# Output projection in two parts: attention heads first, recurrence heads second, in a two-layer fp32 trunk on one core

## The chip, the cores and the metric

One core of a Trainium2 chip runs the whole program as one launch. The metric is the device time in microseconds (us), as a median over runs. PE is the matrix engine, with PEld its weight loads; DVE, ACT and POOL are the vector, scalar and GpSimd engines; SP issues all the DMAs of this kernel.

## The reference

Two layers. In each, the normed input goes through one projection into four attention heads and four gated-recurrence heads. Their outputs, each normed per head, are laid side by side and go through one output projection that is added to the residual; a squared-ReLU MLP follows.

```python
for l in range(DEPTH):                         # DEPTH 2, S = D = 1024
    h = rms_norm(x, norm1_g[l])
    z = h @ w_in[l]                            # split into aq ak av | rq rf ri rg
    oa = diff_attention(...)                   # 4 heads x 128 columns
    orr = hgrn2_chunked(...) * silu(rg)        # 4 heads x 128 columns
    mixed = concatenate([oa, orr], axis=-1)
    x = x + mixed @ w_out[l]                   # the step that is changed
    h2 = rms_norm(x, norm2_g[l])
    u = relu(h2 @ w_up[l])
    x = x + (u * u) @ w_down[l]
return rms_norm(x, final_g)
```

## The kernel before

Everything is held with the model dimension on the 128 partitions: eight blocks `b` of 128 features by two halves `hf` of 512 tokens. A product of fp32 precision is made from three matmuls on split numbers (`hi` and `lo` parts, names `hh`, `hl` for activations, `whi`, `wlo` for weights), so `dense` (L146) with eight blocks is 24 matmuls of 128x512 into one PSUM bank. Those banks come from a pool with the tag `mm`, which has two buffers. `weights` loads a 512 KB piece into `wst` (three buffers), ACT rounds it to `whi` (L130), DVE makes `wlo` (L132), at high priority.

The heads run in pairs, attention head h and then recurrence head h. A scheduler orders the instructions of each engine before the launch, by priority (program order, high priority for evacuations and weights) and its own estimate of when operands are there; at run time each engine takes its list in that order and waits where an operand is missing. So the last attention head and the last recurrence head (`hgrn` with h = 3, output block 7, constant `LAST`) are interleaved. The result of each head goes to DRAM (`mx`), except block 7, which is split at once (L316, L317).

Then comes the output projection. For each half it loads the seven blocks of `mx` into `wst`, splits them into the tiles `hh`, `hl` that the normed input had used, loads the residual blocks `xt[b][hf]` from DRAM (`xs`), and makes eight groups of 24 matmuls, in the block order 0, 4, 1, 5, 2, 6, 3, 7. Each group is added to the residual tile by one DVE instruction (L858). The residual tiles lie in the pool `x`, which is opened after the attention's pool (`actx`) has been closed and takes its memory. After each half comes `norm_rows` (squares on ACT, L188, their sum on DVE, L189, a matmul with ones, L205, an inverse root, giving `R`), and then the scaling (L865) and splitting (L549, L550) of the eight blocks for the MLP, whose first products are the plain ones of `up_plain` (L647): half 0 first, half 1 next.

Of the kernel before, what the change touches and what calls it, by code (L numbers as in the profile page):

```python
# [15 lines left out]
ALU = mybir.AluOpType  # L16
# [4 lines left out]
P = 128  # L21
# [3 lines left out]
NB = D // P  # L25
HALF = 512
NH = 4
# [10 lines left out]
LAST = 2 * NH - 1  # L38
# [7 lines left out]
def trunk(ctx, tc, x, norm1_g, w_in, lam_qk, attn_norm_g, lb_logits, hgrn_norm_g,  # L46
# [3 lines left out]
    V, A, G, T = nc.vector, nc.scalar, nc.gpsimd, nc.tensor  # L50
    dma = nc.sync.dma_start
# [10 lines left out]
    def pst(tag="pa"):  # L62
        return psp.tile([P, HALF], F32, tag=tag, name=tag, bufs=3)
# [11 lines left out]
    xt = {}  # L75
    first = []

    def load_w(src, shape):
        st = wp.tile([P, 1024], F32, tag="wst", name="wst", bufs=3)
        dma(st.rearrange("p (a c) -> p a c", c=shape[1]), src)  # L80
        return st

    with tc.high_priority():
        dma(ident, c_ident)
        dma(rows[0:16], norm1_g.rearrange("l (b p) -> (l b) p", p=P))
        for hf in range(2):
            for dh in range(2):
                t = xp.tile([P, 4, HALF], F32, tag="xt", name="xt", bufs=4)
# [22 lines left out]
    xs = dram.tile([P, NB, S], F32, name="xs")  # L111
# [3 lines left out]
    def h_tiles(b, hf):  # L115
        hi = hp.tile([P, HALF], F32R, tag=f"hh{b}_{hf}", name=f"hh{b}_{hf}")
        lo = hp.tile([P, HALF], F32R, tag=f"hl{b}_{hf}", name=f"hl{b}_{hf}")
        return hi, lo
# [7 lines left out]
    def weights(src, shape, eng=V):  # L126
        with tc.high_priority():
            st = first.pop(0) if first else load_w(src, shape)
            hi = wp.tile([P, 1024], F32R, tag="whi", name="whi")
            A.copy(hi, st)  # L130
            lo = wp.tile([P, 1024], F32R, tag="wlo", name="wlo")
            eng.tensor_tensor(lo, st, hi.bitcast(F32), op=ALU.subtract)  # L132
        r = lambda t: t.rearrange("p (a c) -> p a c", c=shape[1])
        return r(hi), r(lo)

    def dense(w, hs, evac, halves=(0, 1), order=None):
        whi, wlo = w
        order = order or list(range(len(hs)))
        for hf in halves:
            ps = mmp.tile([P, HALF], F32, tag="mm", name="mm")  # L140
            n = 3 * len(order)
            i = 0
            for b in order:
                hi, lo = hs[b][hf]
                for lt, rt in ((whi, hi), (whi, lo), (wlo, hi)):
                    T.matmul(ps, lt[:, b], rt, start=(i == 0), stop=(i == n - 1))  # L146
                    i += 1
            with tc.high_priority():
                evac(hf, ps)
# [86 lines left out]
    for hf in range(2):  # L236
# [6 lines left out]
        for b in range(NB):  # L243
            ps = pst("pa" if b % 2 else "pr")
# [67 lines left out]
    ms = {}  # L312

    def split(src, b, hf):
        hi, lo = h_tiles(b, hf)
        A.copy(hi, src)  # L316
        V.tensor_tensor(lo, src, hi.bitcast(F32), op=ALU.subtract)  # L317
        ms[b, hf] = (hi, lo)
# [445 lines left out]
    for l in range(DEPTH):  # L764
        wl = w_in[l].rearrange("(b p) c -> p b c", p=P)
        rctx, actx, xctx, mctx = ExitStack(), ExitStack(), ExitStack(), ExitStack()
# [5 lines left out]
        for h in range(NH):  # L772
            ap = apool
            Lq = [ap.tile([P, S], F32R, tag=f"L{m}", name=f"L{m}") for m in range(2)]
            Rk = [ap.tile([P, S], F32R, tag=f"R{m}", name=f"R{m}") for m in range(2)]

            def evq(hf, ps):
                sl = slice(hf * HALF, (hf + 1) * HALF)
                t = half(ap, "ta", 1)
                V.tensor_tensor(t, ps, R1[hf], op=ALU.mult)  # L780
                for m in range(2):
                    a, b = slice(64 * m, 64 * m + 64), slice(64 - 64 * m, 128 - 64 * m)
                    A.activation(Lq[m][a, sl], t[a], AF.Copy, scale=-0.125)
                    V.scalar_tensor_tensor(Lq[m][b, sl], t[a], -0.125,
                                           Lq[m][a, sl].bitcast(F32), op0=ALU.mult,
                                           op1=ALU.subtract)

            def evk(hf, ps):
                sl = slice(hf * HALF, (hf + 1) * HALF)
                t = half(ap, "ta", 1)  # L790
                V.tensor_tensor(t, ps, R1[hf], op=ALU.mult)
                for m in range(2):
                    a, b = slice(64 * m, 64 * m + 64), slice(64 - 64 * m, 128 - 64 * m)
                    A.copy(Rk[m][a, sl], t[a])
                    V.tensor_tensor(klo[m][a, sl], t[a], Rk[m][a, sl].bitcast(F32),
                                    op=ALU.subtract)
                    dma(Rk[m][b, sl].bitcast(F32), Rk[m][a, sl].bitcast(F32))

            for base, ev in ((AQ, evq), (AK, evk)):
                c0 = base + P * h  # L800
                dense(weights(wl[:, :, c0:c0 + P], (NB, P), G), hs, ev, order=DONE if l else None)
            if h % 2 == 0:
                va = ap.tile([P, NB, 256], F32, tag="va", name="va", bufs=1)
                dense_rows(wl, AV + P * h, hs, rcol, va)
            vsl = slice(h % 2 * P, h % 2 * P + P)
            attention(l, h, ap, Lq, Rk, klo, va[:, :, vsl])
            ap = rpool
            st = {}
            for nm, base in (("rf", RF), ("rq", RQ), ("rg", RG)):
                st[nm] = [None, None]  # L810

                def ev(hf, ps, nm=nm, ap=ap):
                    if nm == "rq":
                        t = ap.tile([P, 4, P + 64], F32, tag=nm, name=nm, bufs=2)
                        c4 = lambda t: t.rearrange("p (c t) -> p c t", c=4)
                        V.tensor_tensor(t[:, :, 0:P], c4(ps), c4(R1[hf]), op=ALU.mult)
                    else:
                        t = ap.tile([P, HALF], F32, tag=nm, name=nm, bufs=2)
                        V.tensor_tensor(t, ps, R1[hf], op=ALU.mult)
                    st[nm][hf] = t  # L820

                c0 = base + P * h
                dense(weights(wl[:, :, c0:c0 + P], (NB, P), G), hs, ev, order=DONE if l else None)
                if nm == "rf" and h % 2 == 0:
                    vr = ap.tile([P, NB, 256], F32, tag="vr", name="vr", bufs=1)
                    dense_rows(wl, RI + P * h, hs, rcol, vr)
            hgrn(l, h, ap, st, vr[:, :, vsl])
        actx.close()

        xt = [[None, None] for _ in range(NB)]  # L830
        xp = xctx.enter_context(tc.tile_pool(name=f"x{l}", bufs=1))
        order = [0, 4, 1, 5, 2, 6, 3, 7]
        wo = w_out[l].rearrange("(b p) c -> p b c", p=P)
        sctx = ExitStack()
        mp, hst = sctx.enter_context(tc.tile_pool(name=f"sq{l}", bufs=1)), {}
# [1 line left out]
        def xtile(b, hf):  # L837
            return xp.tile([P, HALF], F32, tag=f"x{b}_{hf}", name=f"x{b}_{hf}")

        for hf in range(2):  # L840
            hsl = slice(hf * HALF, (hf + 1) * HALF)
            for i in range(0, NB, 2):
                bb = [b for b in order[i:i + 2] if b != LAST]
                st = wp.tile([P, 1024], F32, tag="wst", name="wst", bufs=3)
                for j, b in enumerate(bb):
                    dma(st[:, j * HALF:(j + 1) * HALF], mx[:, b, hsl])
                    split(st[:, j * HALF:(j + 1) * HALF], b, hf)
            if hf == 1:
                sctx.close()
                rctx.close()  # L850
                mp = mctx.enter_context(tc.tile_pool(name=f"mlp{l}", bufs=1))
            for b in range(NB):
                xt[b][hf] = xtile(b, hf)
                dma(xt[b][hf], xs[:, b, hsl])
            mm = [[ms.get((b, 0)), ms.get((b, 1))] for b in range(NB)]
            for b in range(NB):
                def ev(hf, ps, b=b):
                    V.tensor_tensor(xt[b][hf], ps, xt[b][hf], op=ALU.add)  # L858
                dense(weights(wo[:, :, b * P:(b + 1) * P], (NB, P)), mm, ev, (hf,), order)
            R2 = norm_rows(mp, xt, hf)  # L860
            for b in range(NB):
                dma(xs[:, b, hsl], xt[b][hf])
            for b in (0, 4, 1, 5, 2, 6, 3, 7):
                g0 = 16 + 8 * l + b
                V.scalar_tensor_tensor(xt[b][hf], xt[b][hf], cols[:, g0:g0 + 1], R2, op0=ALU.mult,  # L865
                                       op1=ALU.mult)
                hst[b, hf] = split_into(h_tiles(b, 0) if hf == 0 else form_tiles("B22", b - 4, mp)
                                        if b >= 4 else form_tiles("T4", b, mp), xt[b][hf])
# [178 lines left out]
```

## Time and profile before

| | |
|---|---|
| median of three runs | 2581.79 us (2580.47 to 2583.26) |
| the profiled execution | 2582.39 us, span of its instructions 2580.5 us |
| busy share of the span | PE 96%, PEld 80%, DVE 70%, ACT 49%, POOL 22% |
| mean granted clock of PE | 0.984 of full speed |

PE is busy nearly throughout, so the places to look at are the few in which it waits or runs at the lower of its two clock levels.

### The profile page before, as it was taken

The page shows a single profiled execution, that of the slowest core. Times are in us where ns is not written, and L with a number is a line of the kernel's source. Part 1 is how long each engine was busy: PE and PEld are TensorE (multiplying, and loading weights), DVE is VectorE, ACT ScalarE, POOL GpSimd, SP SyncE. Part 2 cuts the span into 40 slices and gives each one's busy share as a digit, 9 for nine tenths or more (in the row PEclk, how much of TensorE's full clock was granted, in tenths as well). Part 3 has the DMA queues.
Part 4 walks back from the last instruction along what each step waited for, and adds up shares of the span by engine and source line. Part 5 has one row for each costly group of instructions (what it writes and reads, how often), then busy time and mean ns, then how long its engine had stood idle before and what let it go on. Part 6 is the DMA issues. An engine that isn't in the chain of part 4 may idle for free. (4 is left out here: it accounts for less than half of the span.)

```text
span 2580.5 us, 34946 instructions
## 1 busy us (share of the span) xinstructions
PE 2470.6 (96%) x12672; PEld 2053.6 (80%) x12672; DVE 1816.5 (70%) x3205; ACT 1260.5 (49%) x2463; POOL 555.9 (22%) x316
## 2 busy tenths in 40 slices
PE   8999999999999999999999999999899999999997
PEld 6877887777878877888788778877777888778885
DVE  5567756877865668887745785668787565687775
ACT  6455445654555554434434554456545555443433
POOL 1111011001133323333211111110011333333331
PEclk9999999999999999999999999999999999999999
DMA  7121111236354457444311111112554544664532
GB/s 235 47 62 46 46 33 59 74 124 195 127 192 155 151 201 243 145 147 127 115 50 50 42 38 54 38 50 62 165 158 160 175 155 143 240 208 146 157 98 82
DMA packets 254765, 308.96 MB, mean 120 GB/s; under 512 B 14384, under 2 KB 162140, under 8 KB 254592
## 3 DMA queue, kind: packets, MB, share of 16 engines
q1 hardware_dynamic: 254592, 306.73, 36.5%
q8 instruction: 100, 1.64, 0.3%
q14 instruction: 73, 0.60, 0.1%
HBM read 211.75 MB, written 93.08 MB: 118 GB/s over the span
## 5 line engine op out<-in xcount | busy, mean ns | idle before, releaser
L647 PE MATMUL pa<-T,whi 128*128 128x512 f32 x1456 | 457.8, 396 | 11.5 <-issue 4.8
L146 PE MATMUL mm<-hh,whi 128*128 128x512 f32 x896 | 362.4, 405 | 2.3 <-DVE ta L780 1.8
L146 PE MATMUL mm<-hh,wlo 128*128 128x512 f32 x896 | 362.1, 404 | 1.7 <-POOL wlo L132 1.7
L146 PE MATMUL mm<-hl,whi 128*128 128x512 f32 x896 | 361.5, 404 | 0.5 <-DVE hl L123 0.5
L647 PEld LDWEIGHTS pa<-T,whi 128*128 128x128 f32 x1456 | 273.3, 189 | 77.8 <-issue 7.0
L132 POOL TENSOR_TENSOR wlo<-wst,whi 128x1024 fp32r<-128x1024 f32 x56 | 138.8, 2479 | 840.3 <-ACT whi L130 820.7
L624 POOL TENSOR_TENSOR wst<-wr 128x512 f32<-128x512 f32 (+1 forms) x58 | 108.8, 1876 | 943.5 <-DMA wr<-w_down 334.5
L647 PE MATMUL pa<-T,wlo 128*128 128x512 f32 x728 | 286.7, 394 | 0.0
L146 PEld LDWEIGHTS mm<-hh,wlo 128*128 128x128 f32 x896 | 171.6, 191 | 36.6 <-POOL wlo L132 3.9
L146 PEld LDWEIGHTS mm<-hh,whi 128*128 128x128 f32 x896 | 172.0, 192 | 34.5 <-DVE ta L780 2.6
L146 PEld LDWEIGHTS mm<-hl,whi 128*128 128x128 f32 x896 | 172.3, 192 | 33.9 <-DVE hl L123 1.5
L610 ACT CAST whi<-wst 128x1024 fp32r<-128x1024 f32 (+1 forms) x120 | 123.7, 1031 | 139.4 <-PE mm L647 83.7
L611 DVE TENSOR_TENSOR wlo<-wst,whi 128x1024 fp32r<-128x1024 f32 (+1 forms) x120 | 183.4, 1528 | 9.4 <-ACT whi L610 9.1
L610 ACT CAST whi<-wr 128x512 fp32r<-128x512 f32 (+2 forms) x128 | 105.0, 820 | 164.0 <-PE pr L647 136.9
L647 PE MATMUL pr<-hh,whi 128*128 128x512 f32 x456 | 180.7, 396 | 0.0
L647 PE MATMUL pr<-hh,wlo 128*128 128x512 f32 x456 | 179.4, 393 | 0.0
L647 PE MATMUL pr<-hl,whi 128*128 128x512 f32 x456 | 177.7, 390 | 0.0
L611 DVE TENSOR_TENSOR wlo<-wr,whi 128x512 fp32r<-128x512 f32 (+2 forms) x128 | 120.0, 938 | 77.2 <-ACT whi L610 73.3
L647 PEld LDWEIGHTS pa<-T,wlo 128*128 128x128 f32 x728 | 137.2, 189 | 32.9
L514 ACT ACTIVATE s<-s,nm 128x256 f32<-128x256 f32 (+7 forms) x128 | 98.9, 774 | 110.1 <-DVE nm L509 104.5
L224 PE MATMUL mm<-wlo,hh 128*128 128x256 f32 x512 | 146.8, 287 | 0.4 <-POOL wlo L132 0.4
L224 PE MATMUL mm<-whi,hh 128*128 128x256 f32 x512 | 147.2, 287 | 0.0
(297 smaller groups left out, 5710.1 us busy)
## 6 DMA issues: line engine op xcount, KB each, us to landing
us<-us SPq DMA_DIRECT2D x210, 256.0 KB, 2.6
wr<-w_up SPq DMA_DIRECT2D x32, 1024.0 KB, 6.6
wst<-w_in SPq DMA_DIRECT2D x56, 512.0 KB, 3.8
us<-x SPq DMA_DIRECT2D x104, 256.0 KB, 2.4
uf<-us SPq DMA_DIRECT2D x98, 256.0 KB, 2.9
wr<-w_down SPq DMA_DIRECT2D x22, 1024.0 KB
wst<-w_out SPq DMA_DIRECT2D x32, 512.0 KB, 5.2
x<-xs SPq DMA_DIRECT2D x64, 256.0 KB, 4.4
```

The costliest lines, as they stand in the source:

```text
L132: eng.tensor_tensor(lo, st, hi.bitcast(F32), op=ALU.subtract)
L146: T.matmul(ps, lt[:, b], rt, start=(i == 0), stop=(i == n - 1))
L224: T.matmul(ps[:, t * 256:t * 256 + 256], lt[:, tsl], rt[:, b], start=(i + t + b + k == 0), stop=(i == 1 and b == 3 and k == 2), skip_group ...
L514: A.activation(s[:, :nk], s[:, :nk], AF.Exp, bias=nm, scale=-1.0, accum_out=sm)
L610: A.copy(hv, x)
L611: V.tensor_tensor(lv, x, hv.bitcast(F32), op=ALU.subtract)
L624: G.tensor_tensor(sa[:, 0], a21, a22, op=ALU.add)
L647: T.matmul(ps, lt[:, off + j], rt, start=(start and j + i == 0), stop=(j == n - 1 and i == 2), skip_group_check=True)
```

## The change

The output projection becomes `project(b0, hf)`, called four times: blocks 0 to 3 (attention) for both halves, then blocks 4 to 7 (recurrence) for both halves. A group now has 12 matmuls, and there are 32 of them in a layer in place of 16, each added to the residual tile. A weight piece covers four blocks by 256 output columns, still 512 KB, and 16 pieces are still loaded. The residual tiles of both halves are loaded ahead of the first part, and the attention's pool is closed after the last attention head, ahead of the last recurrence head.

```diff
             attention(l, h, ap, Lq, Rk, klo, va[:, :, vsl])
+            if h == NH - 1:
+                actx.close()
...
             hgrn(l, h, ap, st, vr[:, :, vsl])
-        actx.close()
...
-        for hf in range(2):
+        def project(b0, hf):
+
             hsl = slice(hf * HALF, (hf + 1) * HALF)
-            for i in range(0, NB, 2):
-                bb = [b for b in order[i:i + 2] if b != LAST]
+            for i in (0, 2):
+                bb = [b for b in (b0 + i, b0 + i + 1) if b != LAST]
                 st = wp.tile([P, 1024], F32, tag="wst", name="wst", bufs=3)
...
+            mm = [[ms.get((b0 + i, 0)), ms.get((b0 + i, 1))] for i in range(NH)]
+            for d in range(0, NB, 2):
+                w = weights(wo[:, b0:b0 + NH, d * P:(d + 2) * P], (NH, 256))
+                for k in range(2):
+                    def ev(hf, ps, b=d + k):
+                        V.tensor_tensor(xt[b][hf], ps, xt[b][hf], op=ALU.add)
+                    dense([t[:, :, k * P:(k + 1) * P] for t in w], mm, ev, (hf,))
+
+        for hf in range(2):
+            for b in range(NB):
+                xt[b][hf] = xtile(b, hf)
+                dma(xt[b][hf], xs[:, b, hf * HALF:(hf + 1) * HALF])
+            project(0, hf)
+        for hf in range(2):
+            hsl = slice(hf * HALF, (hf + 1) * HALF)
+            project(NH, hf)
             if hf == 1:
                 sctx.close()
                 rctx.close()
                 mp = mctx.enter_context(tc.tile_pool(name=f"mlp{l}", bufs=1))
-            for b in range(NB):
-                xt[b][hf] = xtile(b, hf)
-                dma(xt[b][hf], xs[:, b, hsl])
-            mm = [[ms.get((b, 0)), ms.get((b, 1))] for b in range(NB)]
-            for b in range(NB):
-                def ev(hf, ps, b=b):
-                    V.tensor_tensor(xt[b][hf], ps, xt[b][hf], op=ALU.add)
-                dense(weights(wo[:, :, b * P:(b + 1) * P], (NB, P)), mm, ev, (hf,), order)
             R2 = norm_rows(mp, xt, hf)
```

How the order moves on PE in layer 0, at the end of the first half of the last recurrence head (`L435` are products inside its chunks, `L505`, `L506` attention scores, `L449` its output products). Before, with groups of the output projection (`mm_5716` is the second one):

```order
L506 MATMUL pa_5016<-klo1_479,L1_4545 128x512
L146 MATMUL mm_5716<-hh5_0_5641,whi_5712 128x512
L146 MATMUL mm_5716<-hl5_0_5642,whi_5712 128x512
L146 MATMUL mm_5716<-hh5_0_5641,wlo_5714 128x512
L146 MATMUL mm_5716<-hh2_0_5647,whi_5712 128x512
L146 MATMUL mm_5716<-hl2_0_5648,whi_5712 128x512
L146 MATMUL mm_5716<-hh2_0_5647,wlo_5714 128x512
L146 MATMUL mm_5716<-hh6_0_5652,whi_5712 128x512
L435 MATMUL pr_5390<-X_5385 128x64 x4
```

The second group is spread among them. The same place of PE's list now, where both banks hold their 12 matmuls already (`L529` are attention's transposes):

```order
L506 MATMUL pa_5016<-klo1_479,L1_4545 128x512
L435 MATMUL pr_5391<-X_5386 128x64 x4
L529 MATMUL pa_5029<-ident_82,s_4997 128x128 x4
L529 MATMUL pa_5040<-ident_82,s_4997 128x128 x4
L449 MATMUL pr_5400<-vr_3858,at_5315 128x128
```

No matmul of the projection is left between these. Eighteen rows further down the same list of PE (`L403` and `L425` are first steps of the recurrence head's second half):

```order
L403 MATMUL pr_5498<-rq_5200,tr_5448 128x192 x2
L425 MATMUL pr_5508<-X_5503 64x64 x4
L425 MATMUL pr_5519<-X_5514 32x32 x8
L146 MATMUL mm_5701<-hh0_0_5641,whi_5697 128x512
L146 MATMUL mm_5701<-hl0_0_5642,whi_5697 128x512
```

The third group, `mm_5701`, is the next of the projection, behind the second half's first steps. Counted over the list, 42 matmuls of the output projection stood ahead of block 7's arrival (21 in each of two banks, without block 7), and 24 stand there now (12 in each). Layer 1 has the same counts.

On DVE, the first two additions to the residual now stand behind `L405` of the recurrence head's second half, and free the two banks:

```order
L405 TENSOR_TENSOR at_5492<-pr_5498,ident_82 128x256
L855 TENSOR_TENSOR x0_0_5623<-mm_5667,x0_0_5623 128x512
L855 TENSOR_TENSOR x1_0_5625<-mm_5681,x1_0_5625 128x512
L407 COPY_PREDICATED at_5492<-masks_391,pr_5498 128x128
L415 TENSOR_TENSOR X_5541<-rf_5140,bc_5446 128x32x8
```

Before, `L405` and both `L407` stood ahead of the first such addition, so little moved there on DVE. Further on, at the end of the projection, half 0 is normed and scaled (`L875`, once L865) while half 1 is still added up (`L855`), and now blocks 2, 6 and 3 of half 0 come behind the last addition of half 1:

```order
L855 TENSOR_TENSOR x7_1_5811<-mm_6345,x7_1_5811 128x512
L611 TENSOR_TENSOR wlo_6453<-wr_6446,whi_6452 128x1024
L875 SCALAR_TENSOR_TENSOR x2_0_5627<-x2_0_5627,cols_107,R0_6150 128x512
L875 SCALAR_TENSOR_TENSOR x6_0_5635<-x6_0_5635,cols_107,R0_6150 128x512
L875 SCALAR_TENSOR_TENSOR x3_0_5629<-x3_0_5629,cols_107,R0_6150 128x512
L550 TENSOR_TENSOR hl2_0_6188<-x2_0_5627,hh2_0_6187 128x512
L550 TENSOR_TENSOR hl6_0_6193<-x6_0_5635,hh6_0_6192 128x512
L550 TENSOR_TENSOR hl3_0_6198<-x3_0_5629,hh3_0_6197 128x512
```

Before, all eight blocks of half 0 were split before the fifth of the eight additions of half 1.

## Rows read from the trace of the kernel before

**Rows 1.** The page: the span, and busy time, share and count by engine.
```profile
span 2580.5 us, 34946 instructions
PE 2470.6 (96%) x12672; PEld 2053.6 (80%) x12672; DVE 1816.5 (70%) x3205; ACT 1260.5 (49%) x2463; POOL 555.9 (22%) x316
```
**Rows 2.** Stretches: length, busy PE, PEld, DVE, ACT, POOL, clock, DMA share, GB/s.
```profile
508.00:536.00 28.00, 27.57 (x191) 23.97 (x191) 25.88 (x66) 14.91 (x33) 0.00 (x0) 1.00 0.12 33
540.00:552.00 12.00, 9.18 (x39) 7.83 (x40) 6.98 (x25) 6.14 (x18) 0.00 (x0) 0.57 0.41 140
552.00:636.00 84.00, 83.81 (x410) 69.40 (x409) 66.19 (x98) 40.31 (x69) 8.60 (x4) 1.00 0.67 209
1790.00:1814.00 24.00, 24.00 (x172) 21.12 (x171) 21.23 (x58) 11.31 (x27) 0.00 (x0) 1.00 0.07 21
1820.00:1832.00 12.00, 9.63 (x42) 8.03 (x44) 6.85 (x24) 6.88 (x17) 0.00 (x0) 0.57 0.45 154
```
**Rows 3.** PE in order of time, layer 0: start, length, idle before it and releaser.
```profile
534.29 0.48 PE L146 MATMUL mm<-hh,wlo 128*128 128x512 f32 x1
...
536.21 2.05 PE L534 MATMUL pa<-va,tp 128*128 128x128 f32 x16 [0.44 <-DVE tp L532]
542.14 0.47 PE L474 MATMUL pr<-ident,te 128*128 128x128 f32 x1 [3.88 <-ACT te L473]
...
545.90 2.08 PE L377 MATMUL pr<-vr,tr 128*128 128x128 f32 x8 [0.67 <-ACT tr L371]
...
550.09 0.87 PE L146 MATMUL mm<-hh,whi 128*128 128x512 f32 x1
...
551.59 1.05 PE L425 MATMUL pr<-X 128*64 128x64 f32 x24
```
**Rows 4.** PE in order of time, the same place of layer 1.
```profile
1821.39 1.25 PE L474 MATMUL pa<-ident,tp 128*128 128x128 f32 x4 [5.61 <-ACT tp L473]
...
1825.46 2.08 PE L377 MATMUL pr<-vr,tr 128*128 128x128 f32 x8 [0.98 <-ACT tr L371]
```
**Rows 5.** The instructions of L146 in one stretch: busy PE (count), busy PEld, clock, DMA.
```profile
508.70:535.00 26.30, 11.94 (x42) 7.60 (x42) 1.00 0.09 27
```
**Rows 6.** PE at the end of the output projection, layer 0.
```profile
630.83 0.39 PE L146 MATMUL mm<-hl,whi 128*128 128x512 f32 x1
...
636.49 0.39 PE L146 MATMUL mm<-hh,wlo 128*128 128x512 f32 x1
637.85 0.50 PE L647 MATMUL mm<-hh,whi 128*128 128x512 f32 x1 [0.96 <-ACT whi L610]
```
**Rows 7.** DMA issues of SP, layer 0: start, length of issuing.
```profile
544.50 0.34 SPq L480 DMA_DIRECT2D mx<-tp  x1
546.58 2.71 SPq L854 DMA_DIRECT2D x<-xs  x6
```
**Rows 8.** DVE in order of time, first addition to the residual, layer 0.
```profile
550.58 0.42 DVE L405 TENSOR_TENSOR at<-pr,ident 128x256 f32<-128x256 f32 x1
...
551.47 0.69 DVE L858 TENSOR_TENSOR x<-mm,x 128x512 f32<-128x512 f32 x1
```
**Rows 9.** DVE in order of time, half 0's norm to its last split, layer 0.
```profile
592.39 0.69 DVE L858 TENSOR_TENSOR x<-mm,x 128x512 f32<-128x512 f32 x1 [0.22 <-PE mm L146]
...
602.51 2.08 DVE L865 SCALAR_TENSOR_TENSOR x<-x,cols,R 128x512 f32<-128x512 f32 x3
604.50 0.68 DVE L858 TENSOR_TENSOR x<-mm,x 128x512 f32<-128x512 f32 x1
605.11 0.68 DVE L550 TENSOR_TENSOR hl<-x,hh 128x512 fp32r<-128x512 f32 x1
605.70 1.22 DVE L132 TENSOR_TENSOR wlo<-wst,whi 128x1024 fp32r<-128x1024 f32 x1
606.84 1.28 DVE L550 TENSOR_TENSOR hl<-x,hh 128x512 fp32r<-128x512 f32 x2
...
620.71 1.28 DVE L550 TENSOR_TENSOR hl<-x,hh 128x512 fp32r<-128x512 f32 x2
```

More of the change, by code (lines that the diff above doesn't have):

```diff
@@ L827, in trunk @@
             hgrn(l, h, ap, st, vr[:, :, vsl])
-        actx.close()
         xt = [[None, None] for _ in range(NB)]
         xp = xctx.enter_context(tc.tile_pool(name=f"x{l}", bufs=1))
-        order = [0, 4, 1, 5, 2, 6, 3, 7]
         wo = w_out[l].rearrange("(b p) c -> p b c", p=P)
```

## Prediction

> **What bounds the kernel now.** I read the page first: PE is busy 96% of the span [rows 1], so a change can gain only where PE waits or runs at its lower clock, and it loses wherever it lets PE wait more. Then the busy time by stretches. Between block 7's arrival and the end of the output projection PE is busy 83.81 of 84 us in layer 0 [rows 2]: there is nothing to be filled there. Ahead of it lies a stretch of 28 us in which PE is busy 27.57 and DVE 25.88 [rows 2]; in layer 1 PE 24.00 and DVE 21.23 of 24. There the last attention head, the last recurrence head and 42 matmuls of the projection [rows 5] run side by side. Between the two comes the one hole. PE in order of time shows it: the last projection matmul that can go without block 7 starts at 534.29, PE then waits 3.88 us for ACT's scaling of the heads' outputs and 0.67 us for a copy, and projection matmuls start again at 550.09 [rows 3]. In layer 1 the same two waits are 5.61 and 0.98 us [rows 4]. In the 12 us of each hole the mean granted clock is 0.57 [rows 2]: after the long wait the engine is given the 1.2 GHz level and works through block 7's chain at it. What fills the banks before the hole, and what ends it, is what the change touches.
>
> **The change part by part**, per layer; both layers have the same order, so the sum is doubled.
>
> *Matmuls and weights.* 384 matmuls before, 32 groups of 12 now, again 384; 16 weight pieces of 512 KB before and now. Nothing is removed. At full clock one matmul takes (636.49 - 630.83) / 25 = 0.227 us of PE's time [rows 6].
>
> *a. Less work ahead of the hole.* Before, two banks held 21 matmuls each when PE ran out of work: 42 [rows 5]. Now the two banks hold 12 each, and a third group needs a bank that has been added to its residual tile. That tile's memory was the attention's; its loads stand on SP behind the store of the last attention head's output, which is issued at 544.50, and the loads at 546.58 [rows 7]. So the first addition cannot come before the hole is nearly over, and in DVE's list it stands behind L405, as before at 550.58 [rows 8]. Eighteen matmuls that ran ahead of the hole now run after it, where PE was full: 18 x 0.227 = +4.1 us. The shorter groups thus fill the hole less, not more. Bounds: 0 if the stretch ahead of the hole gets shorter by as much (that is counted in b), 4.1 otherwise; I take 4.1.
>
> The Trainium skill (Perfetto Trace Analysis, section Optimizing Tensor Performance, Matmuls) says that independent groups should rotate through PSUM banks, so that evacuating one overlaps the matmuls of the next. By that rule a would be 0, and the sum below would end 8.2 us lower; the rows of SP and DVE show why the rotation stands still here.
>
> *b. When the hole ends.* Without the 18 matmuls PE is no longer full ahead of it, so DVE sets the pace of the two heads. DVE was idle 28.00 - 25.88 = 2.1 us there [rows 2], so the hole can come at most 2.1 us earlier. Against that, DVE's list has one more weight difference ahead of the hole (L132, 605.70 to 606.84, 1.14 us [rows 9]). Three splits of half 1 (each some 0.6 us, by the like L550, 605.11 to 605.70 [rows 9]) move into the tail of the chain, 1.8 us, while three splits fewer stand at its head. And the third group waits for the addition (0.69 us behind L405 [rows 8]), where before a projection matmul started at 550.09; the products of L425 (1.05 us [rows 3]) stand in that gap now. Bounds: -2.1 + 1.1 = -1.0 to +1.1 + 1.8 + 0.7 = +3.6. DVE's idle time is only in part wait for PE, and the tail was waiting for ACT anyway: I take +0.6.
>
> *c. Clock.* PE's own work of the two heads between 527 and 536 is unchanged, but without the projection matmuls there it is thinner, and the lower clock may come sooner than it did. What it would double: the transposes and products of attention's last block, 2.05 us for L534 [rows 3] and about as much beside it. Bounds 0 to +3; I take +1.
>
> *d. Additions.* 16 more on DVE, (605.11 - 604.50) = 0.61 us each [rows 9]: 9.8 us. DVE is busy 66.19 of 84 us behind the hole [rows 2], so they are covered by PE's matmuls: 0. Without that cover they would cost the 9.8.
>
> *e. Norm of half 0.* Half 0 is complete when only the 96 matmuls of the last call are left: 96 x 0.227 = 21.8 us of cover. Before, its last addition began at 592.39 and PE was busy with half 1 until 636.49 + 0.4: 44.5 us of cover, and the last split of half 0 ended at 620.71 + 1.28 = 622.0, 29.6 us after that addition [rows 6, 9]. DVE's list has between the two, now: 8 additions, 3 weight differences and 2 of the MLP's, 3 sums of squares, 5 steps of the root, 8 scalings (2.0 us for three [rows 9]), 12 splits: 8 x 0.61 + 5 x 1.14 + 3 x 0.6 + 2.8 + 8 x 0.66 + 12 x 0.6 = 27.7 us, before any wait. So the last blocks of half 0 come some 7 us after PE has done with the projection. PE has a first cover: blocks 0 and 1 are split earlier, 12 matmuls of the first two MLP groups (2.7 us), and the others can follow tile by tile, since a tile feeds 6 matmuls (1.4 us) and DVE makes one in about 1.3. PE already waits 0.96 us there [rows 6]. Bounds 0 and +7; I take +1.5. Half 1's norm has the products of half 0 as cover, 96 x 0.227 = 21.8 us, as before.
>
> *f. DMAs.* The eight residual loads of half 1 move ahead of the rest of the weights on SP. Issue takes 2.71 / 6 = 0.45 us each [rows 7], 16 take 7.2 us; the next weight piece behind them is needed after three pieces of matmuls, 72 x 0.227 = 16.3 us, beside the recurrence head's own work: 0, and up to +2 if transfers crowd.
>
> Sum per layer: 4.1 + 0.6 + 1.0 + 0 + 1.5 + 0 = 7.2 us; two layers 14.4 us. On the profiled execution's own 2582.39 us that is 2596.8; the median of the runs is 0.6 us lower, so **2596 us**. Lower bounds in all terms: 4.1 - 1.0 = 3.1 per layer, 2588; upper bounds: 4.1 + 3.6 + 3 + 7 + 2 = 19.7 per layer, 2621.
>
> **The rivals.** A change of 0.2% is 5.2 us, about what a measurement of this kernel can tell from none.
>
> *No change.* The stretch ahead of the hole was bound by PE after all, and 18 matmuls less bring block 7 earlier by their whole 4.1 us; e and c come to nothing. For it: PE had 27.57 of 28 us [rows 2]. Against it: DVE had 25.88, and 2.1 us of room is half of what this needs. It gives 2582, with one of the small terms 2586.
>
> *Faster.* The hole is where this decides: 3.88 + 0.67 us in layer 0 and 5.61 + 0.98 in layer 1 of waiting [rows 3, 4], and half-clock work of 9.18 and 9.63 us busy at 0.57 [rows 2], where full clock would need 5.2 and 5.5 us, so 4 us each. If the residual tiles came early enough that the first part ran through the hole, up to 4.6 + 4.0 + 6.6 + 4.1 = 19 us would go: 2563. It decides when the first addition comes more than the 4.1 us of a ahead of where it came. Against it: the load at 546.58 waits for the attention [rows 7], and PE's list puts the third group behind L425. If half of it came, 2572.
>
> The Trainium skill (Perfetto Trace Analysis, section Optimization Strategy) says that where the most-contended engine changes over time, interleaving the regimes may help; this rival is that rule at work. The trace has the regimes side by side already ahead of the hole.
>
> *Much slower.* DVE's list lets PE wait for half 0 in full: e is 7 in place of 1.5 in both layers, +11 on top of the forecast: 2607, and with c at its bound 2611. For it: DVE was busy 25.88 of 28 us and more work is put into its chains; against it, the list of PE takes matmuls of two groups by turns as tiles come.
>
> **How the numbers follow.** Forecast (slower by 0.2 to 1%) 0.69, no change 0.15, faster 0.08, much slower 0.08. The likeliest one's own range is 2587 to 2607. To leave out no more than 2 in 10 the range takes in most of the no-change case and the first of the much slower one: 2583 to 2609. Slower by over 0.2% is 0.69 + 0.08 = 0.77, within 0.15, faster 0.08.
>
> **What would show it.** In the profile after: 24 projection matmuls ahead of the hole and the first addition at about the place where L858 stood, 551 (a); the hole's length from the last such matmul grown by some 4 us or more; the mean clock around it no higher than 0.57 (c); the stretch behind it full up to the end of the projection, some 5 us later than 636.9 (b); there a wait of PE of 1 to 4 us for a split of half 0 where 0.96 stood (e). Wrong if projection matmuls run between the last attention transposes and L403, if the first addition comes well ahead of 549, or if PE waits within the projection for additions in DVE's list behind the recurrence head's steps.

## The result

The changed kernel takes 2616.42 us (median, 2613.71 to 2619.85); the kernel before took 2582.16 beside it. The ratio is 1.015, 95% interval 1.0132 to 1.0168: slower, by 34 us in the medians, and by 34 to 43 by the interval. The profiled execution has a span of 2618.1 us, 37.6 more than before [rows 1]. The forecast was slower, 2596, with 2609 as the upper end of the range: the sign was right, the size much too small.

### The profile page after: what moved, and what is told of

Its sections match the earlier page's. It is cut to its first block, busy times and chain, and to the rows that moved or that the text cites. A ratio compares the mean times of both kernels' runs of the same rounds, so it can differ in the third digit from the quotient of the medians.

```text
span 2618.1 us, 34979 instructions
## 1 busy us (share of the span) xinstructions
PE 2480.1 (95%) x12672; PEld 2055.6 (79%) x12672; DVE 1842.7 (70%) x3237; ACT 1258.8 (48%) x2463; POOL 555.2 (21%) x316
## 5 line engine op out<-in xcount | busy, mean ns | idle before, releaser
L146 PE MATMUL mm<-hh,wlo 128*128 128x512 f32 x896 | 360.8, 403 | 2.1 <-POOL wlo L132 2.1
L146 PE MATMUL mm<-hh,whi 128*128 128x512 f32 x896 | 360.3, 403 | 2.4 <-DVE ta L780 1.8
L146 PE MATMUL mm<-hl,whi 128*128 128x512 f32 x896 | 359.8, 402 | 0.5 <-DVE hl L123 0.5
L146 PEld LDWEIGHTS mm<-hh,wlo 128*128 128x128 f32 x896 | 170.9, 191 | 36.1 <-POOL wlo L132 4.1
L146 PEld LDWEIGHTS mm<-hh,whi 128*128 128x128 f32 x896 | 171.2, 191 | 34.5 <-DVE ta L780 2.6
L146 PEld LDWEIGHTS mm<-hl,whi 128*128 128x128 f32 x896 | 171.6, 192 | 33.9 <-DVE hl L123 1.5
```

## The profile after

The page's first part, busy time by engine (share of the span) and number of instructions:

```profile
PE 2480.1 (95%) x12672; PEld 2055.6 (79%) x12672; DVE 1842.7 (70%) x3237; ACT 1258.8 (48%) x2463; POOL 555.2 (21%) x316
```

DVE's busy time has grown by some 26 us, of which the 32 additions that came in, at 0.61 us each, are 19.5; PE's has grown by 9.5. To see where 37.6 us went, I cut each layer at the last matmul of the output projection and gave each stretch the same number of PE instructions in both kernels, so that lengths can be compared. Stretches: length, busy PE (count), PEld, DVE, ACT, POOL, mean clock, DMA share, GB/s. First the kernel before: the heads' end with the projection, the norm with the start of the MLP, and both again in layer 1.

```profile
480.10:636.90 156.80, 150.38 (x791) 124.80 (x789) 124.33 (x255) 83.13 (x178) 8.60 (x4) 0.97 0.47 145
636.90:730.00 93.10, 90.63 (x391) 73.22 (x392) 75.10 (x96) 52.95 (x85) 18.32 (x11) 1.00 0.46 159
1740.00:1917.00 177.00, 166.95 (x884) 138.87 (x883) 141.69 (x305) 97.25 (x218) 9.31 (x5) 0.97 0.42 131
1917.00:2020.00 103.00, 100.15 (x431) 80.44 (x431) 76.11 (x99) 56.41 (x92) 21.04 (x12) 1.00 0.47 160
```

The same stretches of the changed kernel:

```profile
482.70:648.30 165.60, 153.23 (x791) 126.95 (x789) 120.92 (x256) 79.67 (x173) 0.00 (x0) 0.96 0.40 131
648.30:755.80 107.50, 94.99 (x391) 74.32 (x392) 90.14 (x112) 54.81 (x91) 26.42 (x15) 0.97 0.44 150
1762.70:1941.00 178.30, 167.15 (x884) 139.04 (x883) 137.35 (x305) 94.79 (x212) 2.40 (x1) 0.97 0.38 124
1941.00:2058.40 117.40, 104.48 (x431) 81.63 (x431) 92.41 (x116) 58.78 (x98) 28.17 (x16) 0.97 0.46 152
```

Heads and projection: +8.8 and +1.3 us. Norm and start of the MLP: +14.4 and +14.4. The four sum to 38.9, the whole of the loss within what the cuts can tell: the three stretches between them differ by +2.6, -3.1 and -0.8 us. A second profile of the changed kernel (the one taken with run 2 below), cut at the same PE instructions, has +6.8 and +1.2, +13.7 and +15.2. So three quarters of it lies behind the projection, where the forecast had put 1.5 us per layer.

The hole in layer 0, PE in order of time (start, length, operation, count, idle before it and releaser), with the first projection matmul behind it; it answers to [rows 3]:

```profile
536.31 0.90 PE L435 MATMUL pr<-X 128*128 128x64 f32 x3 [4.00 <-DVE X L419]
...
549.30 1.25 PE L474 MATMUL pa<-ident,tp 128*128 128x128 f32 x4 [4.49 <-ACT tp L473]
...
553.37 2.07 PE L377 MATMUL pr<-vr,tr 128*128 128x128 f32 x8 [0.98 <-ACT tr L371]
...
557.94 1.02 PE L425 MATMUL pr<-X 128*64 128x64 f32 x24 [0.56 <-DVE S L388]
558.89 0.50 PE L146 MATMUL mm<-hh,whi 128*128 128x512 f32 x1
```

A new wait of 4.00 us stands ahead of the old one: with the banks full, nothing is left for PE while DVE works for the recurrence head. The waits in these rows sum to 10.0 us, those of before to 4.99 [rows 3]. The mean clock falls towards the 1.2 GHz level twice, and is 1.00 between:

```profile
536.00:544.00 8.00, 7.69 (x41) 7.69 (x42) 7.26 (x15) 3.50 (x11) 0.00 (x0) 0.57 0.01 2
...
549.00:560.00 11.00, 9.16 (x57) 7.55 (x58) 6.57 (x19) 4.25 (x12) 0.00 (x0) 0.69 0.60 200
```

Layer 1 has the same new wait, 3.67 us, and the old one behind it is shorter than the 5.61 of before [rows 4]:

```profile
1831.29 1.97 PE L435 MATMUL pr<-X 128*128 128x64 f32 x8 [3.67 <-DVE X L419]
...
1843.50 1.25 PE L474 MATMUL pa<-ident,tp 128*128 128x128 f32 x4 [4.26 <-ACT tp L473]
...
1850.81 1.02 PE L425 MATMUL pr<-X 128*64 128x64 f32 x24 [1.03 <-DVE S L388]
```

With the 0.68 us between the last two, the waits are 9.6 us where they were 6.6.

The loads of the residual come as foreseen, behind the store of the attention head:

```profile
551.39 0.32 SPq L480 DMA_DIRECT2D mx<-tp  x1
553.44 2.69 SPq L861 DMA_DIRECT2D x<-xs  x6
```

Behind the projection, PE (what answers to [rows 6]; the last matmul of the projection starts at 647.89):

```profile
649.24 0.50 PE L647 MATMUL mm<-hh,whi 128*128 128x512 f32 x1 [0.96 <-ACT whi L610]
...
653.72 0.50 PE L647 MATMUL mm<-hl,whi 128*128 128x512 f32 x1 [0.47 <-DVE hl L550]
...
659.62 0.50 PE L647 MATMUL mm<-hl,whi 128*128 128x512 f32 x1 [1.49 <-DVE hl L550]
...
667.21 1.22 PE L205 MATMUL pa<-us,ones 128*128 128x512 f32 x1 [4.05 <-DVE us L189]
...
715.35 0.74 PE L647 MATMUL pa<-T,whi 128*128 128x512 f32 x2 [2.56 <-ACT us L659]
```

and DVE in the same time:

```profile
652.98 1.89 DVE L550 TENSOR_TENSOR hl<-x,hh 128x512 fp32r<-128x512 f32 x3
654.79 0.74 DVE L875 SCALAR_TENSOR_TENSOR x<-x,cols,R 128x512 f32<-128x512 f32 x1
655.45 2.41 DVE L189 TENSOR_TENSOR us<-us 128x512 f32<-128x512 f32 x2
657.78 1.79 DVE L550 TENSOR_TENSOR hl<-x,hh 128x512 fp32r<-128x512 f32 x1
659.49 7.66 DVE L189 TENSOR_TENSOR us<-us 128x512 f32<-128x512 f32 x5
```

The waits for `hl` are the foreseen ones, half 0's splits. The 4.05 us are not: all seven sums of squares of half 1 (L189) stand in DVE's list behind half 0's last scaling, five of them behind its last split too, and the ones-matmul that needs them (L205) stands in PE's list ahead of products of half 0 that could run. In the kernel before, the last of these sums came just behind the projection, whose last matmul started at 636.49 [rows 6]:

```profile
638.97 0.68 DVE L189 TENSOR_TENSOR us<-us 128x512 f32<-128x512 f32 x1
```

Now it ends at 667.15, 19 us behind the projection. The clock pays too, as these stretches of the changed kernel show:

```profile
660.00:668.00 8.00, 3.95 (x15) 2.72 (x14) 6.87 (x5) 0.00 (x0) 5.65 (x4) 0.86 0.01 3
668.00:672.00 4.00, 4.00 (x9) 2.68 (x8) 1.32 (x2) 1.26 (x2) 0.00 (x0) 0.50 0.00 0
```

After the waits PE runs four us at 0.50, the 1.2 GHz level. By the two tables of stretches above, the 14.4 us of layer 0 are 10.0 us more of idle time and 4.4 more of busy time of PE. Of the 10.0, the waits of 0.47, 1.49 and 4.05 us are 6.0; the rest comes at 715 and 720 us, 2.56 and 1.47 us for copies of ACT (L659); in run 3, sums first, these two are gone. What delays these copies was not followed.

## Experiments

Each ratio is to the kernel before on the same chip, with its 95% interval. The kernel before ran there at 2580 to 2582 us in the median, with single runs from 2572 to 2599, so the intervals are wide, 0.002 to 0.003 to each side.

**1. Half by half.** The order of the calls only:

```diff
-            project(0, hf)
         for hf in range(2):
             hsl = slice(hf * HALF, (hf + 1) * HALF)
+            project(0, hf)
             project(NH, hf)
```

> The four calls come in another order: both parts of half 0, its norm, then both parts of half 1. The rest is the changed kernel. Theory A (the norm of half 0 has lost its cover: between the end of the projection and the first product of the MLP's steady part, 62 us went by in place of 52, and 4.5 us more behind it): half 0 is complete 192 matmuls, 43.6 us, ahead of the end again, both layers win back some 14.4 us, and the time is about 2616.4 - 28.8 = 2588; the waits for hl L550 and the 4.05 us for us L189 are gone. Theory B (the loss lies in the shorter groups and the clock around the hole, a to c, and the rest follows from the clock): at least three quarters of the loss stays, 2607 or more.

Measured: 1.0065 (1.0041 to 1.009), 2601.26 us. The loss behind the projection is gone in both layers, stretches as above:

```profile
481.20:653.10 171.90, 156.09 (x791) 128.76 (x789) 131.93 (x271) 82.62 (x178) 5.53 (x4) 0.93 0.41 134
653.10:746.00 92.90, 90.42 (x391) 73.01 (x391) 74.59 (x96) 52.64 (x85) 17.86 (x11) 1.00 0.47 159
1754.70:1940.50 185.80, 169.32 (x884) 140.45 (x883) 148.92 (x321) 98.27 (x218) 7.95 (x5) 0.95 0.39 126
1940.50:2042.80 102.30, 99.84 (x431) 80.67 (x432) 77.21 (x99) 56.53 (x92) 20.84 (x12) 1.00 0.48 162
```

92.9 and 102.3 us, as before the change (93.1, 103.0). Theory A holds for that part. The time did not fall to 2588. The order brings a wait of its own into the projection, one in each layer (run 6 takes it away, and is no faster), here layer 0 on PE:

```profile
631.79 0.79 PE L146 MATMUL mm<-hl,whi 128*128 128x512 f32 x1 [5.51 <-DVE hl L317]
```

The split of one block of half 1 stands in DVE's list behind the scalings of half 0. It is the same mechanism once more.

**2. POOL held.** In the changed kernel the POOL sums of the first `up_pair` step, 1.6 to 2.0 us each, run from 655.30 to 665.8, beside these L189, which take 1.66 us in the median there. The edit makes the first of these POOL sums wait for half 1's inverse root: POOL copies a column of the root into the tile that the sum then overwrites, in the first step alone.

```diff
             if "S" in parts:
                 sa, sb = stile(), stile()
+                if after is not None:
+                    G.tensor_copy(sa[:, 0, 0, 0:1], after[:, 0:1])
...
-            u2 = up_pair(up_forms(q, "AS2"), hB, q, xtile, mp)
+            u2 = up_pair(up_forms(q, "AS2", after=R2 if q == 2 else None), hB, q, xtile, mp)
```

> The changed kernel, with one more instruction: POOL copies a column of the inverse root of half 1 into the tile that its first sum for the MLP overwrites, so POOL's six sums of 1.6 to 2.0 us cannot run beside the sums of squares of half 1 (L189). Theory P (POOL and DVE hold each other up: seven L189 took 10.1 us where seven of 0.61 us are 4.3): L189 falls back to 0.6 us, the ones-matmul's wait of 4.05 us goes, some 4 to 6 us per layer come back, 2604 to 2608. Rival (the place of these sums in DVE's list, behind the scalings and splits of half 0, is what delays it, and the sums for POOL come too late for their products when they are held): 2614 to 2618.

Measured: 1.0119 (1.01 to 1.0138). DVE and PE of this run:

```profile
655.44 3.73 DVE L189 TENSOR_TENSOR us<-us 128x512 f32<-128x512 f32 x5
...
677.40 0.79 PE L649 MATMUL pa<-T,whi 128*128 128x512 f32 x1 [4.57 <-DVE T L550]
```

Five sums take 3.73 us where they took 7.66, and the wait for them is gone, but PE now waits 4.57 us for half 1's splits. Since the ratio left room for a gain, I ran it again beside the changed kernel:

> The changed kernel itself, as the measure for the two runs beside it on this chip: 1.013 to 1.017 times the kernel before.

> The run with POOL's sums held until half 1's inverse root, once more beside the changed kernel. Its first profile showed L189 back at 0.6 to 0.75 us and the wait of 4.05 us gone, but 4.57 us for a split of half 1 in its place, and as much time lost in all (173.8 us against 174.0). Theory (the chain of half 1 on DVE is late with or without POOL): the same ratio as the changed kernel within 0.002. Rival (POOL costs some 4 us per layer after all): 0.003 or more below it.

Measured: the changed kernel 1.014 (1.0114 to 1.0167), with POOL held 1.0145 (1.0118 to 1.0173). Holding POOL brings no time that can be measured. It has not removed the collision, though, but moved it: POOL's sums now run beside half 1's scalings (L877 in this kernel) and splits, here DVE and then POOL of the first of the two runs:

```profile
669.90 5.17 DVE L877 SCALAR_TENSOR_TENSOR x<-x,cols,R 128x512 f32<-128x512 f32 x3
...
667.64 3.51 POOL L626 TENSOR_TENSOR wst<-wr 128x512 f32<-128x512 f32 x2
671.10 3.42 POOL L597 TENSOR_TENSOR wst<-wst,wr 128x512 f32<-128x512 f32 x2
```

Three scalings take 5.17 us where they took 2.08 [rows 9]. Either way DVE loses some 6 us to POOL: the seven sums took 10.1 us, and at 0.61 each are 4.3; held, the six scalings and two splits from 665.08 to 676.67 take 11.6, and at 0.66 and 0.6 each are 5.2. So what the collision costs is not shown; no run had DVE free of it behind the projection with the changed order of calls.

**3. Sums first**, and then both edits together:

```diff
-            R2 = norm_rows(mp, xt, hf)
+            if hf == 1:
+                with tc.high_priority():
+                    R2 = norm_rows(mp, xt, hf)
+            else:
+                R2 = norm_rows(mp, xt, hf)
```

> The changed kernel, with the norm of half 1 (its squares, sums and root) at high priority, so that its sums stand in DVE's list among the last additions, and the scalings and splits of half 0 stand behind them. Theory A' (it is the order of DVE's list that costs: the sums of half 1 all stand behind half 0's splits, and PE's ones-matmul stands ahead of products that could run): the 4.05 us wait and the half-clock stretch behind it go, and the late half 1 with them: 8 us per layer, 2600. Rival (DVE has too much to do in these 22 us, whatever the order): the waits move to the splits of half 0, the time stays within 5 us of 2616.

> Both edits together: half 1's sums early in DVE's list and POOL's sums held behind them. Theory (DVE has the scalings and splits of half 0, the sums of half 1 and the MLP's weights to do in 22 us, so the order alone gives back only part): like the run with the early sums, 1.009, and still above the half-by-half order's 1.0065. Rival (what was left there was POOL's doing, which ran ten us beside DVE): 1.004 to 1.006.

Measured: 1.0091 (1.0061 to 1.012), and together 1.0104 (1.0079 to 1.0129). Sums first gives back 0.005 to 0.006, less than half of the loss; holding POOL adds nothing to it (it moves the collision to half 1's scalings there too). The stretches behind the projection in the first of the two:

```profile
642.30:745.70 103.40, 92.71 (x391) 72.89 (x392) 90.27 (x114) 56.78 (x93) 25.62 (x16) 1.00 0.46 157
...
1925.50:2037.80 112.30, 103.26 (x431) 81.34 (x432) 91.84 (x116) 60.42 (x99) 27.71 (x16) 0.98 0.47 159
```

+10.3 and +9.3 us in place of +14.4 twice. The waits have moved to half 0's splits, the longest 2.73 us. So the order of DVE's list is a part; the rest goes with what DVE still has to do when the projection ends, its time beside POOL included.

**4. The loads alone**, in the unsplit kernel: `actx.close()` ahead of the last recurrence head, and the residual loads of both halves in a loop ahead of the projection.

```diff
+            if h == NH - 1:
+                actx.close()
...
-            for b in range(NB):
-                xt[b][hf] = xtile(b, hf)
-                dma(xt[b][hf], xs[:, b, hsl])
...
```

> The kernel before, unsplit, with only two pieces of the change: the attention's memory is given back ahead of the last recurrence head, and the residual loads of both halves are issued together ahead of the projection. The lists of PE and DVE are those of before, line by line. If the loads cost something (term f, 0 to 2 us per layer) it shows here: theory of the forecast 2582 to 2583; rival, transfers crowd out weights or the parts of mx: 2586 and more.

> The unsplit kernel with the earlier loads once more, in more rounds, since its interval (0.9963 to 0.9999) ended just below 1. If the loads do nothing, the ratio is 1 within 0.001; if they help, 0.997 to 0.999.

Measured: 0.9981 (0.9963 to 0.9999), and in more rounds 0.9999 (0.9979 to 1.0019). The loads cost and bring nothing that can be measured.

**5. Fewer matmuls ahead of the hole**, in the unsplit kernel, in two doses:

```diff
-        order = [0, 4, 1, 5, 2, 6, 3, 7]
+        order = [0, 4, 1, 5, 7, 2, 6, 3]
```

and `[0, 4, 7, 1, 5, 2, 6, 3]`.

> The kernel before, unsplit, with one line changed: block 7 comes fifth in the order of blocks (0, 4, 1, 5, 7, 2, 6, 3), so that a bank can take only 12 matmuls ahead of it, as in the changed kernel, and not 21. Groups, additions, loads and norms are those of before. Theory (terms a to c: the fewer matmuls ahead of the hole are what makes the hole dearer): the time that PE loses between 480 us and the end of the projection, idle or at the lower clock, grows as it did in the changed kernel, by 7.9 us in layer 0 and 4.4 in layer 1, and behind the projection nothing is lost: 2582 + 12 = 2594. Rival (the hole grew by the moved loads, the additions and the shape of the weight pieces, none of which is here): 2585 or less.

> The unsplit kernel before with block 7 third in the order of blocks, so that a bank can take 6 matmuls ahead of it: 12 in place of 42 ahead of the hole (24 with block 7 fifth, which came out at 1.0034). Theory (each matmul that cannot go ahead costs its own time behind the hole): 30 matmuls of 0.227 us per layer, 13.6 us in all if none of it comes back, 1.005. Rival (DVE sets the pace of the two heads, and below some number fewer matmuls cost nothing more): 1.003 as with block 7 fifth.

Measured: 1.0034 (1.0012 to 1.0057) with 24 ahead, 1.0067 (1.0043 to 1.0091) with 12. That is 8.8 us for 36 matmuls fewer in two layers, and 17 us for 60: 0.24 and 0.29 us each (by the intervals 0.09 to 0.41 and 0.18 to 0.39), where a matmul takes 0.227 [rows 6]. The 13.6 us expected of the second lie inside its interval of 11 to 23 us. With 24 ahead, all of it lies ahead of the projection's end, and the norm is as before, here in layer 0:

```profile
486.10:649.20 163.10, 151.90 (x791) 124.66 (x789) 124.73 (x255) 82.72 (x178) 6.90 (x4) 0.97 0.44 140
649.20:742.40 93.20, 90.73 (x391) 73.29 (x392) 74.50 (x96) 52.74 (x86) 17.90 (x11) 1.00 0.46 159
```

That is +6.3 us in layer 0; in layer 1 the same stretch is 179.5 us, +2.5.

**6. Two attempts at a better split.** Half by half, with the splits of half 1 written ahead of half 0's norm; and the same with groups 3 to 5 of the first part in the attention's three banks (`pa`).

```diff
+            if hf == 0:
+                parts(0, 1)
+                parts(NH, 1)
...
+                          bank="pa" if b0 + hf == 0 and d + k in (2, 3, 4) else None)
```

> As the run with the half-by-half order (both parts of half 0, its norm, both parts of half 1), with the loads and splits of half 1's blocks of mixed written ahead of the norm of half 0 and not behind it. Theory (DVE's list follows the written order: there the split of block 6 of half 1 stood behind half 0's scalings and let PE wait 5.5 us in each layer): that wait and the low clock behind it go, what is left over the kernel before is the hole alone, 12.3 us: 2594 to 2596. Rival (the wait is the DMA of those blocks, or it moves to the scalings of half 0): no better than the half-by-half run, 1.0065 times the kernel before, 2599.

> As the run before this one, with groups 3, 4 and 5 of the first part of half 0 put into the three banks that the attention has done with, so that they need not wait for the first residual additions. Theory (the first part stands still for want of banks, term a): some 30 matmuls run ahead of the first addition, the waits of 0.98 and 0.56 us and part of the half-clock stretch are filled, 2 to 4 us per layer come back: 2588 to 2591. Rival (the waits of 4.00 and 4.49 us stand ahead of these groups in PE's list, and they are what the hole costs): within 2 us of the run before.

Measured: 1.0074 (1.0048 to 1.0099) and 1.0075 (1.0047 to 1.0102). The wait of 5.5 us is gone in both, and the time is that of run 1. In its place PE waits for additions, which stand behind half 0's splits, as here in the first of the two:

```profile
637.68 0.47 PE L146 MATMUL mm<-hh,whi 128*128 128x512 f32 x1 [1.16 <-DVE x L856]
...
641.61 0.50 PE L146 MATMUL mm<-hh,whi 128*128 128x512 f32 x1 [0.96 <-DVE x L856]
```

The rivals were nearer. More banks fill only the waits of 0.98 and 0.56 us; the long ones stand ahead of these groups in PE's list, since the attention itself writes `pa` until just behind the second of them:

```profile
544.92 1.25 PE L474 MATMUL pa<-ident,tp 128*128 128x128 f32 x4 [4.50 <-ACT tp L473]
...
547.66 0.78 PE L146 MATMUL pa<-hh,whi 128*128 128x512 f32 x1
```

Banks that are free ahead of the hole were not tried. No split order came within 0.4% of the kernel before at its interval's lower end, so none was found that beats it.

## Why the prediction was wrong, point by point

**a, 18 matmuls deferred, +4.1 us per layer: borne out.** The changed kernel's third group starts at 558.89, behind the loads issued at 553.44. The dose run with 24 ahead gives 4.4 us per layer (8.8 / 2, by its interval 1.6 to 7.4). It holds what follows for hole and clock as well, so it prices a to c together and not a alone.

**b and c, hole and clock, +1.6: right in sum, not in place.** Heads and projection lost 8.8 us in layer 0 and 1.3 in layer 1, 10.1 in all, where a to c forecast 11.4; that the sum fits is in part luck, since 5.7 was forecast for each layer. Both layers show the new wait for DVE, 4.00 and 3.67 us, that I had only as "the lower clock may come sooner". In layer 1 the old wait behind it got shorter, and the kernel before has in this stretch a wait of 1.87 us, at 1787.79, that neither the changed kernel nor the first profile of run 4 shows; so before's 177.0 us are on the long side.

**d, additions covered, 0: right while the projection lasts** in the changed kernel, which shows no wait of PE for an addition there. The cover is thin: the better splits of run 6 wait for additions.

**e, +1.5: the step that failed.** It measured 14.4 us in each layer, 28.8 of 38.9. Half 0's part was near: its last split ends at 659.57, 11 us behind the projection where I had some 7, and PE waits 0.47 and 1.49 us for its splits. What was wrong is the sentence "Half 1's norm has the products of half 0 as cover, 96 x 0.227 = 21.8 us, as before". Before, half 1's sums were done 3 us after the projection, because half 0's scalings and splits had long left DVE's list. Now they stand behind them, so half 1's sums are done 19 us after the projection, some 16 later, and the cover is used up by DVE's lateness with half 0. I had summed DVE's list, half 1's eight additions included, only as far as half 0's last split, and put nothing behind it: half 1's seven sums, its root and its eight scalings and splits come there. Nor did I count that the seven sums would run beside POOL's and take 10.1 us. Run 1 shows the cover to be the cause: given 192 matmuls of it again, the whole loss behind the projection goes. Run 3 shows that reordering alone gives a third of it back there. Run 1 also puts POOL's first sums back under the projection (633 to 641 us, with its end at 653), so it does not part DVE's own list from its time beside POOL.

**f, the loads, 0: right**, as far as the unsplit kernel can tell (run 4).

**The rivals.** Much slower, 2607 to 2611, was the nearest, with a chance of 0.08; it too priced half 0 alone. Faster stayed out, and the rows fit the reason given, that the first part cannot rotate before the residual comes; no run had the residual earlier than the attention's end. The rule of the Trainium skill that independent groups should rotate through PSUM banks (Perfetto Trace Analysis, section Optimizing Tensor Performance, Matmuls) was not enough here: with three more banks (run 6), which come free only in the hole, the ratio did not move. Its rule on interleaving regimes (section Optimization Strategy) was not borne out by any order tried.

What stays open: the split orders of runs 1 and 6 stand 0.003 to 0.004 above the dose run with the same 24 matmuls ahead, with overlapping intervals; their profiles show waits for splits and additions, but which of them makes the difference was not separated. Nor is it known how much of the 14.4 us would go if POOL's sums ran where DVE has time.

## What to carry to other kernels

When a loop over halves is turned inside out, so that each half ends later and both end together, add up the vector engine's list for both halves between the last evacuation and the first need, not for the first half alone. What was hidden behind the other half's matmuls then falls on the end, and an in-order engine lets the second half's short sums wait behind all of the first half's splits. A shorter accumulation group puts less work ahead of a hole when no further bank comes free there: with 24 and 12 matmuls ahead in place of 42, the unsplit kernel took 1.0034 and 1.0067 times as long.

## What the hardware showed that was not expected

DVE and POOL hold each other up. The sums of half 1 in the changed kernel, by their line (count, ns as shortest/median/longest, first and last start):

```profile
L189 DVE TENSOR_TENSOR us<-us x7: 683/1660/1782, 655.4 to 666.5; 128x512 f32<-128x512 f32 x7
```

Beside POOL's sums one took 1.66 us in the median, the shortest 0.68; with POOL held, five took 3.73 us, 0.75 each. A POOL sum took 1.59 to 2.00 us there, and 1.27 and 1.29 us in run 1 at 633.33 and 634.69, where DVE was mostly idle. The Trainium skill (SBUF — State Buffer, section SBUF: two separate sides) says that such a DVE operation and a POOL operation that reads SBUF take a shared pair of ports in turns, each for a whole instruction; the trace agrees, since a sum then takes about as long as a POOL sum. The kernel before has the same collision, but under the projection's matmuls, where PE does not wait for it:

```profile
623.64 4.11 DVE L189 TENSOR_TENSOR us<-us 128x512 f32<-128x512 f32 x3
```

In the changed kernel it lies behind the projection, on the chain that PE waits for.
